# The RWKV-7 scans of a two-layer block: products with state and values on quarters of the array, a state update in two parts, and another order of the pieces

## The chip, the cores and the metric

One core of one Trainium2 chip runs the whole block: an RWKV-7 mixer (layer 0), then a differential-attention mixer (layer 1), over 2048 latent tokens and 256 context tokens of width 1024, all in float32. The metric is the device time of the launch in microseconds (us). The engines in the text are TensorE (PE; its weight loads are the rows PEld), VectorE (DVE), ScalarE (ACT), GpSimd (POOL) and SyncE (SP), whose queue issues most DMAs.

## The reference, cut to the scans

```python
def wkv_scan(r, w, k, v, kk, a, s0, reverse):
    def step(S, inp):                                   # per head: S is 64 x 64
        r_t, w_t, k_t, v_t, kk_t, a_t = inp
        sa = jnp.einsum("bhvk,bhk->bhv", S, kk_t)
        S = (S * w_t[:, :, None, :] - sa[..., None] * (kk_t * a_t)[:, :, None, :]
             + v_t[..., None] * k_t[:, :, None, :])
        return S, jnp.einsum("bhvk,bhk->bhv", S, r_t)
    s_fin, o = lax.scan(step, s0, xs, reverse=reverse)
...
    oc_f, sc_f = scan_direction(con, 0, s0, False)      # context, forwards and backwards
    oc_b, sc_b = scan_direction(con, 1, s0, True)
    ol_f, _ = scan_direction(lat, 0, sc_f, False)       # latents, from the context's final states
    ol_b, _ = scan_direction(lat, 1, sc_b, True)
    y = rwkv7_readout(ol_f + ol_b, lat, r_k, gn_g, gn_b, w_out, h.dtype)
```

There are 16 heads of width 64, two directions, and 2304 tokens in each scan.

## The kernel before, in words

`phase1` (to about 1150 us) projects and writes per-chunk operands to HBM, `phase2` (about 1168 to 2355 us) does the scans, and the readout, the attention and the output projection follow. Only `phase2` is touched.

A scan is done in 36 chunks of 64 tokens, both directions in step, so that each chunk has 32 head-and-direction problems of 64x64 blocks. Partitions 0-63 are `LO`, 64-127 `HI`; `half[d]` is the half of direction d, `other[d]` the other one. The loop `for m in range(nch + LEAD)` does the part of chunk m that needs no state, and the part with the state, `chain`, for chunk i = m - 5:

- `products` (L669) multiplies keys and queries of chunk m, 64x64 weights, 128 columns, on the four quarters of the array in turn. `scores_k` masks two such blocks into `KS` (DVE, L676), `scores_b` copies `A` (ACT, L681) and masks `Pb` (DVE, L682). Each call fills both banks of the pool `sc`.
- `invert` turns the 32x32 diagonal blocks of `A`, for a pair of chunks: four transposes on DVE (L692), then 30 elimination steps on GpSimd (L699, L700). `unpack` transposes the result back on DVE; `join_rows` (L728) and `join` (L744) build the full inverse `U` on TensorE, after a negation of `Dg` on DVE (L737). Their results pass through `sc` banks and are copied by ACT (L730, L746).
- `chain` stage 1 (L766): `KS` times the values, 128 columns of weights, into one bank for each head half and direction (`x00` to `x11`). Stage 2 (L775): queries times the state `St`, added in the same banks, and four ACT copies into `RS` (L783). Stage 3 (L790): `U` times that, with four ACT negations (L794). Stage 4 (L802): the keys turned by `turned` (L754) times the whole column of `RS`, 128 rows of weights, and DVE adds and decays the state (L804, L805). Stage 5 (L811): `Pb` times the result, four ACT copies (L814), DMA out.
- `seen` (L768) is a DVE copy of one element: other rows of the array add to the same banks in stage 2, so the first product there waits for it.

PE, DVE, ACT and POOL run in the order in which the program is written (`in_order`); SP's order is the scheduler's. Odd i and even i differ: for odd i the inverse of the next pair is unpacked and `join_rows` runs, for even i the two `join`s finish and `A` of a new pair is inverted. So the program repeats every two chunks. From m = 36 on there are no scores, and `fill` puts pieces of another product between the stages.

Of the kernel before, what the change touches and what calls it, by code (L numbers as in the profile page):

```python
# [612 lines left out]
def phase2(k):  # L613
# [9 lines left out]
    with ExitStack() as st:  # L623
# [5 lines left out]
        pp = pool("p2p", LEAD)  # L629
# [3 lines left out]
        rp = pool("p2r", 2)  # L633
        sc = pool("p2sc", 2, space=PSUM)
        xo = pool("p2xo", 1, space=PSUM)
# [3 lines left out]
        U = cx.tile([128, 32, 64], F32, name="U")  # L639
        St = cx.tile([128, 2, NPAIR, 64], F32, name="St")  # L640
# [11 lines left out]
        def values(i):  # L652

            RS = []
            for d in range(2):
                t = rp.tile([128, 16, 64], F32, name=f"RS{d}")
                n = ORDER[d][i]
                nc.sync.dma_start(out=t[other[d]], in_=S["v"][64 * n:64 * n + 64].rearrange("t (h v) -> t h v", v=64))
                RS.append(t)
            return RS  # L660

# [24 lines left out]
        def invert(A, eng):  # L686

            N = ip.tile([128, 32, 32], F32, name="N", bufs=2)
            for g in range(4):
# [7 lines left out]
            for m in range(1, 31):  # L697
                t = ip.tile([128, 31 - m, m], F32, name="rank1")
                eng.tensor_tensor(t, bcast(N[:, m + 1:32, m], 2, m), bcast(N[:, m, 0:m], 1, 31 - m), op=ALU.mult)  # L699
                eng.tensor_tensor(N[:, m + 1:32, 0:m], N[:, m + 1:32, 0:m], t, op=ALU.subtract)  # L700
                if eng is nc.vector and m % 5 == 0:
                    yield
            nc.gpsimd.memset(N.rearrange("p i j -> p (i j)")[:, 0:1024:33], -1.0)
            yield N

# [13 lines left out]
        joint = lambda: (sc if more else ch).tile([128, 16, 32], F32, name="scps" if more else "chps")  # L719
# [37 lines left out]
        def chain(i, QR, KS, Pb, RS, KB):  # L757
# [3 lines left out]
            px = [[xo.tile([128, 8, 64], F32, name=f"x{ab}{d}") for d in range(2)] for ab in range(2)]  # L761
            for p in range(8):
                for ab in range(2):
                    for d in range(2):
                        h = 8 * ab + p
# [5 lines left out]
            QR = both(QR, i)  # L771
            for d in range(2):
                for p in range(8):
                    for ab in range(2):
                        nc.tensor.matmul(px[ab][d][:, p], f2(QR[d][half[ab], p]), St[half[ab], d, p], start=False,  # L775
                                         stop=False, skip_group_check=True)
                        if (d, p, ab) == (0, 0, 0):
                            k.tc.add_manual_dep(
                                nc.cur_bb.bb.instructions[-1], before.name,
                                mybir.DependencyInfo(mybir.DependencyClass.Sync, mybir.DependencyReason.DATA),  # L780
                                reason="other rows of the array have added to the same banks")
                for ab in range(2):
                    nc.scalar.copy(RS[d][half[d], 8 * ab:8 * ab + 8], px[ab][d][LO])  # L783
            yield
            pa = [ch.tile([128, 8, 64], F32, name="chps") for _ in range(2)]
            for ab in range(2):
                for p in range(8):
                    for d in range(2):
                        h = 8 * ab + p
                        nc.tensor.matmul(pa[ab][half[d], p], U[half[d], 16 * par + h], RS[d][half[d], h], start=(p == 0),  # L790
                                         stop=True, skip_group_check=True)
            for d in range(2):
                for ab in range(2):
                    nc.scalar.mul(RS[d][half[d], 8 * ab:8 * ab + 8], pa[ab][half[d]], -1.0)  # L794
            yield
            if not last:
                KB = both(KB, i)
                for d in range(2):
                    ps = ch.tile([128, 8, 64], F32, name="chps")
                    for p in range(8):  # L800
                        for ab in range(2):
                            nc.tensor.matmul(ps[half[ab], p], KB[d][:, p, ab], RS[d][:, 8 * ab + p], start=(p == 0),  # L802
                                             stop=True, skip_group_check=True)
                    nc.vector.tensor_tensor(St[:, d], ps, St[:, d], op=ALU.add)  # L804
                    nc.vector.tensor_tensor(St[:, d], St[:, d], bcast(k.dec[:, d, ORDER[d][i]], 2, 64), op=ALU.mult)  # L805
            yield
            for ab in range(2):
                for p in range(8):
                    for d in range(2):
                        h = 8 * ab + p  # L810
                        nc.tensor.matmul(px[ab][d][HI, p], Pb[half[d], h], RS[d][half[d], h], start=False, stop=True,  # L811
                                         skip_group_check=True)
                for d in range(2):
                    nc.scalar.copy(RS[d][other[d], 8 * ab:8 * ab + 8], px[ab][d][HI])  # L814
            for d in range(2):
                n = ORDER[d][i]
                (nc.sync if i + 2 < NCH else nc.scalar).dma_start(
                    out=S["o"][d, 64 * n:64 * n + 64].rearrange("t (h v) -> t h v", v=64), in_=RS[d][other[d]])
# [5 lines left out]
        QR, KS, Pb, BK, BT, RS, KB, A = {}, {}, {}, {}, {}, {}, {}, {}  # L824
# [7 lines left out]
        turn = itertools.cycle((("RS0", rp), ("RS1", rp)))  # L832

        def spare():

            name, pool = next(turn)
            return pool.tile([128, D], F32, name=name)
# [5 lines left out]
        banks = itertools.cycle(f"x{ab}{d}" for ab in range(2) for d in range(2))  # L843

        def modulations(parts, space, pool, name):

            bank = lambda: pool.tile([128, 512], F32, name=name())
# [4 lines left out]
        if k.mod:  # L852
            mods = [modulations(((0, 4, 6), (1, 4, 6)), spare, xo, lambda: next(banks)),
                    modulations(((1, 0, 4),), free, sc, lambda: "scps")]
        inv0, unp, joins, N, chains = none, none, [none, none], {}, {}

        def first(A):
            for N[0] in invert(A, nc.vector):
                yield

        with in_order(k, mybir.EngineType.PE, mybir.EngineType.DVE, mybir.EngineType.Activation, mybir.EngineType.Pool):
            for m in range(nch + LEAD):
# [22 lines left out]
                if 0 <= i + 1 < nch:  # L885
                    RS[i + 1] = values(i + 1)
# [8 lines left out]
                odd = i >= 0 and i % 2 == 0  # L895
                if even:
# [4 lines left out]
                if more:  # L901
                    KS[m] = kp.tile([128, 16, 2, 64], F32, name="KS")
                    scores_k(0, both(BK, m), both(QR, m), KS[m])
# [4 lines left out]
                if more:  # L908
                    scores_k(1, both(BK, m), both(QR, m), KS[m])
                fill()  # L910
                if even:
# [3 lines left out]
                step(c)  # L915
                fill()
# [7 lines left out]
                if more:  # L924
                    if par == 0:
                        A[g] = ip.tile([128, 32, 64], F32, name="A", bufs=2)
                    Pb[m] = pp.tile([128, 16, 64], F32, name="Pb")
                    scores_b(0, both(BK, m), both(QR, m), A[g], Pb[m], par)
                if even:
                    step(unp)  # L930
                turn_keys(0)
                fill()
                if more:
                    scores_b(1, both(BK, m), both(QR, m), A[g], Pb[m], par)
# [7 lines left out]
                if 0 <= i + 1 < nch:  # L942
                    chains[i + 1] = chain(i + 1, QR, KS.pop(i + 1), Pb.pop(i + 1), RS.pop(i + 1), KB)
                    step(chains[i + 1])
                turn_keys(1)
                if more and par == 1:
                    if g == 0:
                        inv0 = first(A[0])
                    else:
                        for N[g] in invert(A[g], nc.gpsimd):  # L950
# [771 lines left out]
```

## Time and profile before

| | |
|---|---|
| median of 3 runs | 5145.27 us (5145.12 to 5148.8) |
| profiled execution | 5129.72 us, its span 5128.0 us |
| scans, first product to last chunk | 1168 to 2355 us |
| PE busy in the span | 92% |
| mean granted TensorE clock | 0.941 of full speed, 0.85 from 1400 to 2200 us |

A row of the profile gives an engine's busy time, its operation and tiles, and in brackets how long the engine was idle ahead of it and what released it. On PE one product in float32 is two rows, each with a weight load, so "x64" is 32 products; the text calls such a load and product a pair. A PEld row shows best when pairs are issued, since the rows of PE overlap.

### The profile page before, as it was taken

The numbers are of one execution on the slowest core, as the hardware profiler recorded it, in microseconds if no ns is written. First come the engines' busy times: TensorE is split into PE (matmuls) and PEld (weight loads), VectorE is DVE, ScalarE is ACT, GpSimd is POOL, SyncE is SP. The second block draws the span as 40 slices with busy tenths as digits, with TensorE's granted clock in tenths as the row PEclk, the third lists the DMA queues.
The fourth block names the chain that finished last, engine by engine and source line by source line (L and its number), as shares of the span: only waits on it lengthen the run. The fifth ranks groups of instructions, "written<-read, shape, count | busy, mean of one in ns | idle before, by whom it ended". The sixth has DMA issues, their size and how long they took to land. (4 is left out here: it accounts for less than half of the span.)

```text
span 5128.0 us, 103635 instructions
## 1 busy us (share of the span) xinstructions
PE 4706.2 (92%) x43090; PEld 4207.0 (82%) x43090; DVE 3582.4 (70%) x5478; ACT 2452.0 (48%) x4170; POOL 1458.2 (28%) x1809
## 2 busy tenths in 40 slices
PE   7999999994888888896878999998999999999999
PEld 5999999992878787875667888887888988888887
DVE  6778777774555555556887628517899989899853
ACT  5555555550434444343333122215777777777730
POOL 1221112111555555551331112113233223223310
PEclk8999999996888888898889999998999999999999
DMA  4565564555444444455654232231110111010042
GB/s 169 159 185 169 165 186 150 174 156 190 139 145 139 137 134 140 145 153 184 209 185 144 97 125 93 99 105 33 28 35 27 28 44 35 10 44 17 9 152 91
DMA packets 610965, 593.39 MB, mean 116 GB/s; under 512 B 27014, under 2 KB 525113, under 8 KB 609473
## 3 DMA queue, kind: packets, MB, share of 16 engines
q1 hardware_dynamic: 608337, 584.15, 36.8%
q8 instruction: 340, 5.57, 0.5%
q10 hardware_dynamic: 2160, 2.62, 0.2%
q14 instruction: 128, 1.05, 0.1%
HBM read 386.91 MB, written 199.77 MB: 114 GB/s over the span
## 5 line engine op out<-in xcount | busy, mean ns | idle before, releaser
L1454 ACT ACTIVATE p<-p,m 128x2304 f32<-128x2304 f32 x256 | 568.8, 2222 | 203.2 <-DVE p L1443 200.9
L1486 PE MATMUL pv<-v,at 128*128 128x128 f32 x4608 | 626.5, 277 | 6.3 <-ACT at L1481 4.6
L1486 PEld LDWEIGHTS pv<-v,at 128*128 128x128 f32 x4608 | 564.3, 192 | 16.1 <-ACT at L1481 12.9
L1440 PE MATMUL sc<-ks,qh 128*128 128x512 f32 (+1 forms) x1280 | 520.6, 407 | 15.3 <-DVE p L1443 15.2
L1441 PE MATMUL sc<-ks,ql 128*128 128x512 f32 (+1 forms) x1280 | 464.2, 372 | 0.3 <-POOL ql L1421 0.3
L363 PE MATMUL mmps<-hH,wH 128*128 128x386 f32 x1632 | 432.6, 345 | 19.1 <-DVE sg L574 12.8
L1464 DVE SCALAR_TENSOR_TENSOR p<-p,r,p 128x1152 f32<-128x1152 f32 x256 | 427.1, 1669 | 4.5
L363 PE MATMUL mmps<-hL,wH 128*128 128x386 f32 x1632 | 428.1, 342 | 2.1 <-DVE hL L92 2.1
L1481 ACT COPY at<-tps 128x512 f32<-128x512 f32 (+1 forms) x640 | 345.2, 540 | 177.4 <-PE tps L1479 174.0
L363 PE MATMUL mmps<-hH,wL 128*128 128x386 f32 x1632 | 427.1, 342 | 1.2 <-DVE nm_ss L197 0.8
L967 PE MATMUL mmps<-wH,hH 128*128 128x512 f32 x1088 | 425.0, 391 | 3.1 <-ACT hH L91 3.1
L967 PE MATMUL mmps<-wL,hH 128*128 128x512 f32 x1088 | 424.8, 390 | 0.0
L967 PE MATMUL mmps<-wH,hL 128*128 128x512 f32 x1088 | 424.3, 390 | 0.0
L1443 DVE TENSOR_SCALAR_CACHE_REDUCE p<-sc,m 128x1280 f32<-128x1280 f32 x256 | 395.6, 1545 | 18.0 <-PE sc L1441 1.4
L1421 POOL TENSOR_TENSOR ql<-qt,qh 128x256 fp32r<-128x256 f32 x128 | 112.2, 877 | 979.1 <-ACT qt L1420 917.8
L1479 PE MATMUL tps<-ident,p 128*128 128x128 f32 x2304 | 361.8, 275 | 10.6 <-ACT qt L1420 5.0
L669 PE MATMUL scps<-QR,BK 64*64 64x128 f32 x4608 | 250.1, 332 | 125.2 <-DVE KS L676 31.4
L1443 DVE TENSOR_SCALAR_CACHE_REDUCE p<-sc 128x1024 f32<-128x1024 f32 x256 | 311.7, 1218 | 56.7 <-PE sc L1441 55.6
L669 PEld LDWEIGHTS scps<-QR,BK 64*64 64x64 f32 x4608 | 185.9, 166 | 176.6 <-DVE KS L676 41.7
L1479 PEld LDWEIGHTS tps<-ident,p 128*128 128x128 f32 x2304 | 273.1, 141 | 61.3 <-ACT at L1481 11.7
L363 PEld LDWEIGHTS mmps<-hH,wH 128*128 128x128 f32 x1632 | 299.2, 192 | 24.9 <-DVE sg L574 16.3
L363 PEld LDWEIGHTS mmps<-hH,wL 128*128 128x128 f32 x1632 | 302.3, 191 | 2.1 <-DVE wL L92 2.0
(296 smaller groups left out, 10427.4 us busy)
## 6 DMA issues: line engine op xcount, KB each, us to landing
wr<-in_rw_in_dram SPq DMA_DIRECT2D x102, 512.0 KB
s_qr<-QR SPq DMA_DIRECT2D x48, 768.0 KB
QR<-s_qr SPq DMA_DIRECT2D x72, 512.0 KB
BK<-s_bk SPq DMA_DIRECT2D x72, 512.0 KB
BT<-s_bk SPq DMA_DIRECT2D x72, 512.0 KB
s_bk<-BK SPq DMA_DIRECT2D x47, 768.0 KB
wraw<-in_da_in_dram SPq DMA_DIRECT2D x64, 512.0 KB
RS<-s_v SPq DMA_DIRECT2D x72, 256.0 KB
```

What stands on the lines that cost most here:

```text
L363: nc.tensor.matmul(a[:, :b1 - b0], wt[:, kt, :], ht[:, kt, b0:b1], start=(kt == 0 and wt is wH and ht is hH), stop=(kt == KT - 1 and last))
L669: nc.tensor.matmul(f2(out[ab][(other if key else half)[d], j]), BK[d][rows, p, 1 - d if key else d], f2(QR[d][rows, p]), start=(j == 0), s ...
L967: k.nc.tensor.matmul(ps, s(kt), m(kt), start=(kt == 0 and s is sH and m is mH), stop=(kt == KT - 1 and last))
L1421: nc.gpsimd.tensor_tensor(ql, qt, qh.bitcast(F32), op=ALU.subtract)
L1440: nc.tensor.matmul(s[:, b0 - g0:b1 - g0], qh[:, cs], ks, start=True, stop=False)
L1441: nc.tensor.matmul(s[:, b0 - g0:b1 - g0], ql[:, cs], ks, start=False, stop=True)
L1443: nc.vector.tensor_scalar(tiles[n][c][:, g0:g1], s[:, :g1 - g0], -1.0, m, op0=ALU.mult, op1=ALU.min, accum_out=least)
L1454: nc.scalar.activation(P, P, AF.Exp, bias=m, scale=-1.0, accum_out=z)
L1464: nc.vector.scalar_tensor_tensor(P0[:, b0:b1], P1[:, b0:b1], r, P0[:, b0:b1], op0=ALU.mult, op1=ALU.add)
L1479: nc.tensor.transpose(ps[:, c - b0:c - b0 + 128], P0[:, c:c + 128], k.ident)
L1481: (eng.copy if eng is nc.scalar else eng.tensor_copy)(at[b][:, :b1 - b0], ps[:, :b1 - b0])
L1486: nc.tensor.matmul(acc, at[b][:, c - b0:c - b0 + 128], H.v[:, c // 128], start=(c == 0), stop=(c == T - 128))
```

## The change

- Stages 1 and 2 take 64 columns of weights at a time (`slot` 0 and 1), so that four quarters of the array are in use in turn. The banks are by head half and by slot: `px` (pool `xp`, rows `half[d]`, the part that goes on) and `po` (pool `op`, rows `other[d]`, the output). Two ACT copies of 128 partitions go to a new tile `RU`.
- Stage 4 takes 64 rows of weights at a time, in two parts: with the values, ahead of stage 3, and with `RU`, after it. It uses the two `xps` banks that `px` has left, which stage 1 of the next chunk takes again.
- `RS0`, `RS1` become one tile `RV` of two buffers; ACT does the three evacuations in two copies each instead of four.
- The negation of `Dg` goes from DVE to ACT. The joins always use `ch` banks.
- In odd m `scores_b` is now ahead of `scores_k`, `invert` starts in mid-iteration with its transposes spread out, and its first four elimination steps are on DVE.

```diff
         def invert(A, eng):
...
-                    yield
+                    yield N
+            yield from eliminate(nc.vector, 1, 5)
+            yield from eliminate(eng, 5, 31)
             nc.gpsimd.affine_select(out=N, in_=N, pattern=[[1, 32], [-1, 32]], base=-1, channel_multiplier=0,
...
-        joint = lambda: (sc if more else ch).tile([128, 16, 32], F32, name="scps" if more else "chps")
+        joint = lambda: ch.tile([128, 16, 32], F32, name="chps")
...
-                nc.vector.tensor_scalar(U[r, cs, 32 * (g % 2):32 * (g % 2) + 32], Dg[r, cs], -1.0, None,
-                                        op0=ALU.mult)
+                nc.scalar.mul(U[r, cs, 32 * (g % 2):32 * (g % 2) + 32], Dg[r, cs], -1.0)
...
-                        nc.tensor.matmul(px[ab][d][:, p], f2(KS[other[d], h]), RS[d][other[d], h], start=(p == 0),
-                                         stop=False, skip_group_check=True)
-            nc.vector.tensor_copy(seen, px[1][1][:, 7, 0:1])
+                        add(t[ab][rows[d], p], KS[other[d], h, slot], RV[other[d], h], p == 0, False)
+            nc.vector.tensor_copy(seen, po[1][:, 7, 0:1])
...
+            for slot, (t, rows) in enumerate(((px, half), (po, other))):
                 for p in range(8):
+                    for d in range(2):
+                        for ab in range(2):
+                            add(t[ab][rows[d], p], QR[i, d][half[ab], p, slot], St[half[ab], d, p], False, slot == 0)
...
+                if slot == 0:
                     for ab in range(2):
+                        nc.scalar.copy(RU[:, 8 * ab:8 * ab + 8], px[ab])
+            yield
+            if not last:
+                pS = [xp.tile([128, 8, 64], F32, name="xps") for _ in range(2)]
+                for p, ab, h in heads:
+                    for d in range(2):
+                        add(pS[d][half[ab], p], KB[i, d][other[d], p, ab], RV[other[d], h], p == 0, False)
...
             if not last:
-                KB = both(KB, i)
+                for p, ab, h in heads:
+                    for d in range(2):
+                        add(pS[d][half[ab], p], KB[i, d][half[d], p, ab], RU[half[d], h], False, True)
...
+                    rest = [lambda q=q: scores_b(q, *args, A[g], Pb[m], par) for q in range(2)]
+                    order = rest + keys if par else keys + rest
```

On PE, stage 1 of a chunk before (`x` are its banks, `RS` the values; one row is one product):

```order
L669 MATMUL scps_16298<-QR_15540,BK_15833 64x128
L766 MATMUL x00_16326<-RS0_15984,KS_14270 128x64
L766 MATMUL x01_16327<-RS1_15986,KS_14270 128x64
L766 MATMUL x10_16328<-RS0_15984,KS_14270 128x64
L766 MATMUL x11_16329<-RS1_15986,KS_14270 128x64
```

and the same stage in the changed kernel, where every product of the chain stands at L765:

```order
L669 MATMUL scps_22481<-QR_21606,BK_21931 64x128
L765 MATMUL xps_22509<-RV_22110,KS_20069 64x64 x2
L765 MATMUL ops0_22511<-RV_22110,KS_20069 64x64 x2
L765 MATMUL xps_22510<-RV_22110,KS_20069 64x64 x2
L765 MATMUL ops1_22512<-RV_22110,KS_20069 64x64 x2
```

Each product of 128 columns has become two of 64, the two directions (x2) into one bank, and the two slots into different banks.

On ACT, an even i before, from the copies of stage 2 to those behind the second `join`:

```order
L783 COPY RS_16864<-x_17206 64x512
L783 COPY RS_16864<-x_17208 64x512
L783 COPY RS_16866<-x_17207 64x512
L783 COPY RS_16866<-x_17209 64x512
L746 COPY U<-scps 32x16x32 x2
L794 ACTIVATE RS_16864<-chps 64x512 x2
L794 ACTIVATE RS_16866<-chps 64x512 x2
L814 COPY RS_16864<-x_17206 64x512
L814 COPY RS_16866<-x_17207 64x512
L814 COPY RS_16864<-x_17208 64x512
L814 COPY RS_16866<-x_17209 64x512
L746 COPY U<-scps 32x16x32 x2
```

and in the changed kernel:

```order
L742 ACTIVATE U<-Dg 32x16x32 x4
L759 COPY KB_23636<-chps 128x512 x2
L790 COPY RU<-xps 128x512 x2
L750 COPY U<-chps 32x16x32 x2
L681 COPY A<-scps 128x256 x2
L803 ACTIVATE RU<-chps 128x512 x2
L681 COPY A<-scps 128x256 x2
L817 COPY RV<-ops_23569 128x512
L817 COPY RV<-ops_23570 128x512
L742 ACTIVATE U<-Dg 32x16x32 x4
L750 COPY U<-chps 32x16x32 x2
```

The three evacuations are two rows each, and the four negations stand behind the output's copies and ahead of `U`'s.

On DVE, an even i before, from the state's update to the next mask (`N` is the block to invert):

```order
L805 TENSOR_TENSOR St<-St,dec 128x512
L737 TENSOR_SCALAR U<-Dg 32x16x32 x4
L682 TENSOR_TENSOR Pb<-scps,causalP 128x256 x4
L768 COPY seen<-x_15838 128x1
L692 STREAM_TRANSPOSE N<-A 32x1024 x2
L692 STREAM_TRANSPOSE N<-A 32x32x32 x2
L676 TENSOR_TENSOR KS<-scps,causalK 128x512 x2
```

and in the changed kernel:

```order
L682 TENSOR_TENSOR Pb<-scps,causalP 128x256 x4
L701 STREAM_TRANSPOSE N<-A 32x1024
L810 TENSOR_TENSOR St<-xps,St 128x512
L811 TENSOR_TENSOR St<-St,dec 128x512
L810 TENSOR_TENSOR St<-xps,St 128x512
L811 TENSOR_TENSOR St<-St,dec 128x512
L701 STREAM_TRANSPOSE N<-A 32x1024
L676 TENSOR_TENSOR KS<-scps,causalK 128x512 x2
L701 STREAM_TRANSPOSE N<-A 32x32x32
L676 TENSOR_TENSOR KS<-scps,causalK 128x512 x2
L774 COPY seen<-ops_15588 128x1
L701 STREAM_TRANSPOSE N<-A 32x32x32
```

The four transposes no longer stand in a row, and the negation is gone from this queue.

## Rows read from the trace of the kernel before

**Rows 1.** Stretches: length, busy PE, PEld, DVE, ACT, POOL, granted clock, DMA share, GB/s.
```profile
1168.00:1287.00 119.00, 67.38 (x842) 39.07 (x842) 62.79 (x111) 11.60 (x28) 16.50 (x31) 0.64 0.48 166
1400.00:2200.00 800.00, 698.50 (x15505) 639.09 (x15499) 448.98 (x552) 329.66 (x632) 425.15 (x814) 0.85 0.46 140
1804.73:1808.38 3.65, 3.65 (x67) 3.65 (x64) 0.76 (x2) 0.65 (x2) 0.00 (x0) 1.00 0.69 185
1839.97:1846.88 6.91, 6.91 (x64) 6.90 (x64) 0.00 (x0) 1.06 (x2) 6.05 (x11) 0.50 0.38 132
2200.00:2355.00 155.00, 139.87 (x2827) 116.50 (x2825) 60.32 (x76) 68.37 (x125) 54.24 (x103) 0.91 0.51 156
```

**Rows 2.** Groups by line and shape, 1400 to 2200 us: busy, mean ns, idle before.
```profile
L775 PEld LDWEIGHTS x<-St,QR 64*128 64x128 f32 x1664 | 118.1, 227 | 28.0 <-DVE seen L768 25.8 <-issue 2.2
L737 DVE TENSOR_SCALAR U<-Dg 32x512 f32<-32x512 f32 x104 | 59.6, 573 | 1.9
L814 ACT COPY RS<-x 64x512 f32<-64x512 f32 x105 | 61.0, 581 | 97.6 <-PE x L811 95.7
```

**Rows 3.** Blocks of one kind, from the timeline: start, duration, pairs, at the granted clock there.
```profile
1801.35 0.86 PEld L669 LDWEIGHTS scps<-QR,BK 64*64 64x64 f32 x30 [1.14 <-ACT U L746]
1802.38 0.86 PEld L754 LDWEIGHTS chps<-ident,BT 128*128 128x128 f32 x8 [0.17 <-issue]
1804.73 3.65 PEld L766 LDWEIGHTS x<-RS,KS 64*128 64x128 f32 x64 [0.17 <-issue]
1809.47 3.65 PEld L775 LDWEIGHTS x<-St,QR 64*128 64x128 f32 x64 [0.17 <-issue]
1814.02 2.00 PEld L790 LDWEIGHTS chps<-RS,U 64*64 64x64 f32 x64
1824.78 2.10 PEld L728 LDWEIGHTS scps<-Tt,A 32*32 32x32 f32 x128
1839.97 6.91 PEld L775 LDWEIGHTS x<-St,QR 64*128 64x128 f32 x64 [1.97 <-DVE seen L768]
1858.15 1.95 PEld L811 LDWEIGHTS x<-RS,Pb 64*64 64x64 f32 x64
2250.04 1.95 PEld L802 LDWEIGHTS chps<-RS,KB 128*64 128x64 f32 x64 [1.34 <-ACT RS L794]
```

**Rows 4.** Who waited for whom, 1400 to 2200 us: total us, times, longest.
```profile
PEld scps L669 <- ACT U L746: 28.5, 26, 1.1
PEld scps L669 <- DVE KS L676: 26.2, 26, 1.6
PEld x L775 <- DVE seen L768: 25.8, 13, 2.1
PEld scps L669 <- ACT Tt L730: 21.9, 25, 1.1
PEld scps L744 <- PE x L811: 11.2, 13, 0.9
PEld chps L802 <- ACT RS L794: 9.6, 13, 0.7
PEld scps L744 <- DVE U L737: 3.3, 13, 0.3
POOL N L695 <- DVE N L692: 313.1, 13, 26.7
```

**Rows 5.** The second join of an even i, from the timeline.
```profile
1859.33 2.40 ACT L814 COPY RS<-x 64x512 f32<-64x512 f32 x4 [2.76 <-PE x L811]
1860.00 1.74 DVE L737 TENSOR_SCALAR U<-Dg 32x512 f32<-32x512 f32 x4
1860.95 0.14 PEld L744 LDWEIGHTS scps<-U,Tt 32*32 32x32 f32 x2 [0.86 <-PE x L811]
```

More of the change, by code (lines that the diff above doesn't have):

```diff
@@ L755, in turned, with chain @@
                 nc.scalar.copy(KB[:, 4 * q:4 * q + 4], ps.rearrange("p j (a c) -> p j a c", a=2))
-        def chain(i, QR, KS, Pb, RS, KB):
+        def chain(i, QR, KS, Pb, RV, KB):
             last = i + 1 == NCH
             par = i % 2
-            px = [[xo.tile([128, 8, 64], F32, name=f"x{ab}{d}") for d in range(2)] for ab in range(2)]
-            for p in range(8):
-                for ab in range(2):
+            add = lambda out, lhsT, rhs, start, stop: nc.tensor.matmul(out, lhsT, rhs, start=start, stop=stop,
+                                                                        skip_group_check=True)
+            heads = [(p, ab, 8 * ab + p) for p in range(8) for ab in range(2)]
+            px = [xp.tile([128, 8, 64], F32, name="xps") for _ in range(2)]
+            po = [op.tile([128, 8, 64], F32, name=f"ops{ab}") for ab in range(2)]
+            for p, ab, h in heads:
+                for slot, (t, rows) in enumerate(((px, half), (po, other))):
@@ L770, in chain @@
             yield
-            QR = both(QR, i)
-            for d in range(2):
+            for slot, (t, rows) in enumerate(((px, half), (po, other))):
                 for p in range(8):
-                    for ab in range(2):
[L775 to L783, printed above, removed]
@@ L784, in chain @@
-            yield
+                    for d in range(2):
+                        for ab in range(2):
+                            add(t[ab][rows[d], p], QR[i, d][half[ab], p, slot], St[half[ab], d, p], False, slot == 0)
+                            if before:
+                                k.tc.add_manual_dep(
+                                    nc.cur_bb.bb.instructions[-1], before.name,
+                                    mybir.DependencyInfo(mybir.DependencyClass.Sync, mybir.DependencyReason.DATA),
+                                    reason="other rows of the array have added to the same banks")
+                                before = None
@@ L810, in chain @@
                         h = 8 * ab + p
[L811 to L814, printed above, removed]
+                        add(po[ab][other[d], p], Pb[half[d], h], RU[half[d], h], False, True)
+                nc.scalar.copy(RV[:, 8 * ab:8 * ab + 8], po[ab])
             for d in range(2):
@@ L831, in phase2 @@
         both = lambda t, i: [t[i, d] for d in range(2)]
-        turn = itertools.cycle((("RS0", rp), ("RS1", rp)))
         def spare():
-            name, pool = next(turn)
-            return pool.tile([128, D], F32, name=name)
+            return rp.tile([128, D], F32, name="RV")
         def free():
             return bp.tile([128, D], F32, name="BK")
-        banks = itertools.cycle(f"x{ab}{d}" for ab in range(2) for d in range(2))
         def modulations(parts, space, pool, name):
-            bank = lambda: pool.tile([128, 512], F32, name=name())
+            bank = lambda: pool.tile([128, 512], F32, name=name)
             for layer, lo, hi in parts:
@@ L852, in phase2 @@
         if k.mod:
-            mods = [modulations(((0, 4, 6), (1, 4, 6)), spare, xo, lambda: next(banks)),
-                    modulations(((1, 0, 4),), free, sc, lambda: "scps")]
+            mods = [modulations(((0, 4, 6), (1, 4, 6)), spare, xp, "xps"),
+                    modulations(((1, 0, 4),), free, sc, "scps")]
         inv0, unp, joins, N, chains = none, none, [none, none], {}, {}
-        def first(A):
-            for N[0] in invert(A, nc.vector):
-                yield
         with in_order(k, mybir.EngineType.PE, mybir.EngineType.DVE, mybir.EngineType.Activation, mybir.EngineType.Pool):
@@ L895, in phase2 @@
                 odd = i >= 0 and i % 2 == 0
+                if more:
+                    KS[m] = kp.tile([128, 16, 2, 64], F32, name="KS")
+                    Pb[m] = pp.tile([128, 16, 64], F32, name="Pb")
+                    if par == 0:
+                        A[g] = ip.tile([128, 32, 64], F32, name="A", bufs=2)
+                    args = both(BK, m), both(QR, m)
+                    keys = [lambda q=q: scores_k(q, *args, KS[m]) for q in range(2)]
+                    rest = [lambda q=q: scores_b(q, *args, A[g], Pb[m], par) for q in range(2)]
+                    order = rest + keys if par else keys + rest
+                else:
+                    order = [lambda: None] * 4
                 if even:
@@ L900, in phase2 @@
                     step(joins[0])
-                if more:
-                    KS[m] = kp.tile([128, 16, 2, 64], F32, name="KS")
-                    scores_k(0, both(BK, m), both(QR, m), KS[m])
+                order[0]()
                 fill()
@@ L907, in phase2 @@
                 step(c)
-                if more:
-                    scores_k(1, both(BK, m), both(QR, m), KS[m])
+                order[1]()
                 fill()
+                if more and par == 1:
+                    inv = invert(A[g], nc.gpsimd if g else nc.vector)
+                    N[g] = step(inv)
                 if even:
@@ L914, in phase2 @@
                 fill()
-                step(c)
-                fill()
+                if more and par == 1:
+                    step(inv)
                 if even:
@@ L923, in phase2 @@
                     step(joins[1])
[L924 to L928, printed above, removed]
+                order[2]()
                 if even:
                     step(unp)
+                if more and par == 1:
+                    step(inv)
                 turn_keys(0)
                 fill()
+                order[3]()
                 if more:
-                    scores_b(1, both(BK, m), both(QR, m), A[g], Pb[m], par)
                     for d in range(2):
@@ L947, in phase2 @@
                     if g == 0:
-                        inv0 = first(A[0])
+                        inv0 = inv
                     else:
-                        for N[g] in invert(A[g], nc.gpsimd):
+                        for _ in inv:
                             pass
```

52 lines of the change are left out of this document (22 added, 30 removed).

## The prediction

> **What bounds the kernel now.** I read the stretches first. From 1400 to 2200 us PE is busy for 698.5 of 800 us, VectorE for 449, ScalarE for 330, GpSimd for 425, and DMA for a share of 0.46 [rows 1]. So the scans are PE's, with two leaks: PE idles for 12% of the time, and its granted clock is 0.85. The groups give the period: 1664 pairs of stage 2 are 26 chunks of 64 pairs, so a chunk takes 800/26 = 30.8 us [rows 2].
>
> Then I read what such a chunk is made of. [...] The sum is 20.7 us. The seven waits of the load queue add up to 126.5 us in 26 chunks, which is 4.9 us each [rows 4]. [...] That makes 30.2; the other 0.6 us are short idles at changes of shape. The reader is to see that two thirds of a chunk is issuing, and that the waits and the clock share the rest.
>
> **What the products on quarters change.** What sets a block's length is how many parts of the array work at a time. With 64 columns of weights, 64 pairs take 2.00 us in stage 3 (two row halves, one bank), 1.95 in stage 5 (the same), and 1.95 in stage 4 (two column halves) [rows 3]: two at a time, so a quarter needs 2 x 1.95/64 = 61 ns per pair. The scores show four at a time: 30 pairs of twice the moving columns take 0.86 us, 29 ns each, which is 115 ns for a quarter [rows 3]; two at a time that would be some 57 ns. Four quarters at 61 ns make 15.2 ns per pair. No row has four quarters at 64 moving columns. The bounds are 15.2 and the 30.5 ns of two at a time. I take 15.2: 128 pairs of joins go in 2.10 us, 16.4 ns each [rows 3], so issuing at that rate is shown.
>
> Stages 1, 2 and 4 go from 64 pairs each to 128, so from 3.65 + 3.65 + 1.95 = 9.25 us to 3 x 1.95 = 5.85 us. That takes 3.4 us off a chunk, and 17.3 us of issuing are left. That stage 4's first half runs ahead of stage 3 costs nothing more, as it is in this count. Its new wait, for `xps` banks that ScalarE must have emptied, is covered by the second slot and a block of scores (0.98 + 0.92 us against two copies of 0.58 [rows 2]).
>
> [...]
>
> **What the order and the queues change, per chunk.** (a) Scores waited for `U` and `Tt`, since the joins used their banks: 28.5 + 21.9 us in 26 chunks, 1.9 each [rows 4]. The joins now use `ch`, whose next user stands behind a block of scores. I take 0. If that cover were too short, the uncovered part of a second copy of 0.58 would return. (b) The waits for `KS` and for `seen`, 1.0 each [rows 4], stay: VectorE's transposes are spread out, but PE arrives earlier. (c) Stage 4's wait of 9.6/26 = 0.4 falls to 0.2, as one negation is left behind stage 3 where there were three. (d) The second join of an even i gets a longer wait. Now VectorE negates beside ScalarE's output copies, and PE waits 0.86 us [rows 5], 14.5 us in all, 0.6 a chunk [rows 4]. In the changed queue ScalarE first makes the last output copy (0.58) and then three negations that the product needs. ScalarE's price for these isn't in the trace; VectorE's are 0.44 (four in 1.74 us [rows 5]) to 0.573 [rows 2], and a copy of 512 columns on ScalarE is 0.58. With 0.3 for the product to land that is 2.2 to 2.6 us, so 1.3 a chunk. PE has nothing to do meanwhile; behind the join stand scores and the turned keys. (e) `join_rows` waits for two transposes of `unpack`, which now come late since PE is ahead: between 0 and one transpose (2 us in two chunks, about 1.0 a chunk). I take 0.3, nearest to today's nothing. (f) The four elimination steps on VectorE, the new RV buffers and the early start of `invert` are on engines with room: GpSimd waits 313 of 800 us for its transposes [rows 4]. Their cover is VectorE's idle 44%; without it the steps would add to (b). DMA goes from a share of 0.46 to about 0.55, and stays hidden unless a key block, loaded as the last scores end, takes longer than what PE does until the next scores, some 4.8 us (1.95 + 0.86 + 1.95).
>
> The waits then are 1.0 + 1.0 + 0.2 + 1.3 + 0.3 = 3.8 us.
>
> **The sum.** (17.3 + 3.8 + 0.6) / 0.85 = 25.5 us, 5.2 less than the 30.7 of today. The clock stays at 0.85 in it, since issuing and waiting shrink alike: waits were 5.5 of 26.2 us at full clock and will be 4.4 of 21.7. There are 31 chunks with scores: 161 us. The last five (155 us in [rows 1], with the clock at 0.91) save 3.4 less the longer join wait, 2.6 each: 13 us. The first five iterations (119 us, where PE is busy for 67) have no `chain`; I leave them. So 174 us go. The profiled execution took 5129.7 us (its span 5128.0 and 1.7 around it), 15.5 under the median of 5145.3; 5129.7 - 174 = 4956, and with that distance **4970 us**.
>
> **The rivals.** *The clock falls.* [...] At a mean of 0.75 a chunk is 21.7/0.75 = 28.9 us, and the gain 1.8 x 31 + 13 = 69 us: 5076. For it speaks that the clock falls here after stretches with waits (0.85 against 0.91 in the end [rows 1]); against it that the share of waits falls from 21% to 20%. *The waits go.* If the spread transposes take `KS` and `seen` away, (b) and (e) are 0.8 in place of 2.3 and the clock may rise to 0.92: (17.3 + 2.3 + 0.6)/0.92 = 22.0, so 5145 - 8.7 x 31 - 13 = 4862. *Only two quarters at a time (slower).* If the quarters of one row half take turns, the pair costs 30.5 ns, the three stages 11.7 us, 2.5 more than before, and with today's waits all 36 chunks lose 2.5/0.85 = 2.9: 5145 + 106 = 5251. With my waits (1.1 fewer) it is 1.6 a chunk, 5204. At my waits it decides from (9.25 + 1.1)/384 = 27 ns a pair. For it speaks that no row has four quarters at 64 columns, and that both row halves now write to one bank in stage 1; against it that stage 3 does that at 2.00 us, where stage 4, from one row range, takes 1.95 [rows 3]. [...] *ScalarE's queue binds.* If each join and each evacuation waits behind negations, and (d) doubles and (e) reaches its bound, the waits are 5.8 and a chunk (17.3 + 5.8 + 0.6)/0.85 = 27.9 us; the gain is 2.8 x 31 + 13 = 100 us: 5045.
>
> **How the numbers follow.** My forecast holds with 0.6 (4920 to 5010, by 24 to 27 us a chunk), the falling clock 0.11, the waits going 0.12, ScalarE's queue 0.10, two at a time 0.07. The range leaves out the slower case and the far end of the good one: 4885 to 5080. A difference of 0.2%, 10 us, is about what a measurement here can tell from none: faster 0.91, the same 0.03 (27 ns a pair or near), slower 0.06.
>
> **What would show it.** In the changed profile 64 pairs of a quartered stage should take about 1 us in the load queue at full clock, 2 us if I am wrong. Scores should no longer wait for `U` or `Tt`, and the second join should wait some 2.5 us for ScalarE's negation once in two chunks. The chunk should be 25.5 us, the clock near 0.85, and the last five chunks about 2.6 us shorter each. A pair at 27 ns or more, or a clock under 0.75, makes the prediction wrong, and so does a wait for loads of `BK`, of which the trace has none from 1400 us on.

## The result, and the profile after

The changed kernel takes 5063.45 us (median of 4 runs, 5055.34 to 5065.65) against 5145.19 for the kernel before on the same chip (4 runs), a ratio of 0.9838 with a 95% interval of 0.9821 to 0.9855. That is 82 us less, in the direction of the forecast and inside its range, but less than half of the 175 us forecast. The profiled execution has a span of 5053.6 us.

The stretches, with the columns of [rows 1]:

```profile
1168.00:1287.00 119.00, 70.68 (x1298) 44.50 (x1296) 66.12 (x122) 19.73 (x44) 29.47 (x53) 0.71 0.49 161
1400.00:2200.00 800.00, 619.56 (x21738) 565.66 (x21730) 442.58 (x577) 325.91 (x608) 412.65 (x753) 0.87 0.50 149
2200.00:2355.00 155.00, 98.57 (x2091) 75.66 (x2086) 78.35 (x111) 52.28 (x83) 19.62 (x13) 0.80 0.58 181
```

From 1400 to 2200 us PE is busy for 620 us, where it was 699, in which it does 40% more products; so it idles for 180 us, where it idled for 101. The waits of its load queue in that stretch, with the columns of [rows 4], say for what:

```profile
PEld xps L765 <- issue: 49.7, 57, 3.2
PEld ops L765 <- issue: 48.4, 28, 5.6
PEld chps L748 <- ACT U L742: 36.7, 28, 2.1
PEld scps L669 <- issue: 29.4, 30, 4.0
PEld chps L748 <- issue: 16.0, 6, 3.5
PEld chps L758 <- issue: 13.0, 29, 2.4
PEld chps L733 <- issue: 7.5, 9, 1.6
PEld xps L765 <- DVE seen L774: 7.0, 8, 1.0
PEld scps L669 <- DVE KS L676: 1.6, 8, 0.3
```

The scores' waits for `U` and `Tt` [rows 4] are gone, those for `KS` and `seen` nearly. In their place stands "issue": PE waits for nothing that the profile can name, for 169 us in all, single times for 5.6. The timeline shows where (start, duration, pairs, idle before):

```profile
1801.95 0.73 PEld L669 LDWEIGHTS scps<-QR,BK 64*64 64x64 f32 x25 [1.34 <-issue]
1802.55 1.11 PEld L765 LDWEIGHTS xps<-RU,KB 64*64 64x64 f32 x63
...
1803.60 1.19 PEld L765 LDWEIGHTS ops<-RU,Pb 64*64 64x64 f32 x37
1805.97 0.83 PEld L765 LDWEIGHTS ops<-RU,Pb 64*64 64x64 f32 x25 [1.18 <-issue]
1808.90 0.18 PEld L748 LDWEIGHTS chps<-U,Tt 32*32 32x32 f32 x2 [2.11 <-ACT U L742]
```

63 pairs of a quartered stage take 1.11 us at a granted clock of 1.00, close to the forecast (64 in about 1 us). But the stops for "issue" stand in the middle of blocks, between pairs that depend on nothing new.

The first row below is the last output copy ahead of that join, the second the negation behind it (ScalarE's timeline, against [rows 5]):

```profile
1806.97 0.58 ACT L817 COPY RV<-ops 128x512 f32<-128x512 f32 x1 [1.64 <-PE ops L765]
1807.58 2.57 ACT L742 ACTIVATE U<-Dg 32x512 f32<-32x512 f32 x4
```

The next table puts the main profiled runs side by side. A chunk is a 31st of the time from the first stage 1 to the 32nd; the granted clock and the "issue" idles of the load queue are those from 1400 to 2000 us, the idles divided by the chunks in them. The ratio is to the kernel before on the same chip.

| kernel | ratio, 95% | first stage 1 | chunk us | "issue" us a chunk | clock |
|---|---|---|---|---|---|
| before | 1 | 1286.9 | 30.65 | 1.0 | 0.85 |
| changed | 0.984 (0.982-0.986) | 1270.6 | 28.71 | 6.1 | 0.86 |
| order only | 0.964 (0.961-0.967) | 1263.4 | 25.69 | 0.9 | 0.96 |
| quarters only | 0.998 (0.997-1.000) | 1287.5 | 30.06 | 4.9 | 0.85 |
| changed, stage 4 whole | 0.971 (0.969-0.974) | 1270.4 | 26.64 | 4.3 | 0.92 |
| changed, earlier negation | 0.976 (0.974-0.978) | 1275.2 | 27.47 | 5.8 | 0.90 |
| changed, two quarters at a time | 0.988 (0.985-0.990) | 1267.3 | 29.14 | 3.7 | 0.94 |
| changed, more traffic | 0.994 (0.991-0.996) | 1279.5 | 30.15 | 6.8 | 0.85 |
| order only, more traffic | 0.974 (0.972-0.977) | 1265.6 | 26.88 | 1.9 | 0.93 |

Of the 74 us in the span, 16 come before the first stage 1, 60 from the 31 chunks; the four chunks after them, which run without scores, lose 7 (102.6 us before, 109.3 after), and the rest of the program gains the remainder.

### The profile page after: what moved, and what is told of

Its sections match the earlier page's. It is cut to its first block, busy times and chain, and to the rows that moved or that the text cites. A ratio compares the mean times of both kernels' runs of the same rounds, so it can differ in the third digit from the quotient of the medians.

```text
span 5053.6 us, 117000 instructions
## 1 busy us (share of the span) xinstructions
PE 4542.8 (90%) x49938; PEld 4055.6 (80%) x49938; DVE 3536.9 (70%) x5470; ACT 2422.7 (48%) x4098; POOL 1412.2 (28%) x1673
## 5 line engine op out<-in xcount | busy, mean ns | idle before, releaser
L1443 PE MATMUL sc<-ks,qh 128*128 128x512 f32 (+1 forms) x1280 | 520.1, 406 | 15.3 <-DVE p L1446 15.2
L693 POOL TENSOR_TENSOR rank<-N 128x130 f32<-128x130 f32 (+14 forms) x442 | 234.2, 530 | 419.8 <-DVE N L694 386.5
L363 PEld LDWEIGHTS mmps<-hL,wH 128*128 128x128 f32 x1632 | 299.9, 190 | 3.3 <-DVE hL L92 3.1
```

Of the source, the lines that this page charges most:

```text
L363: nc.tensor.matmul(a[:, :b1 - b0], wt[:, kt, :], ht[:, kt, b0:b1], start=(kt == 0 and wt is wH and ht is hH), stop=(kt == KT - 1 and last))
L1443: nc.tensor.matmul(s[:, b0 - g0:b1 - g0], qh[:, cs], ks, start=True, stop=False)
```

## The experiments

**One part at a time.** The order only: the changed kernel with `chain` as before, on `RS` and the four `x` banks.

```diff
-                        add(t[ab][rows[d], p], KS[other[d], h, slot], RV[other[d], h], p == 0, False)
+                        nc.tensor.matmul(px[ab][d][:, p], f2(KS[other[d], h]), RS[d][other[d], h], start=(p == 0),
+                                         stop=False, skip_group_check=True)
```

> The new order, the joins' banks and ScalarE's negation of Dg, with stages 1, 2 and 4 whole as before (592 pairs a chunk instead of 784). Theory S (the engine runs out of instructions: in the changed kernel PE idles 126.5 us of 600 for nothing that the profile names, 6.0 us in each of 21 chunks, and a chunk of 784 pairs takes 28.7 us, 36.6 ns a pair): 592 pairs at 36.6 ns are 21.7 us, so the instructions hardly bind here; the waits that went (1.9 for U and Tt, less 0.7 more for Dg) come off, a chunk is 30.65 - 1.2/0.85 = 29.2 us, the prefix gains the same 16 us, and the whole is about 5145 - 45 - 16 = 5085, ratio 0.988 to the kernel before. Rival R (the quarters gave their 3.4/0.85 = 4.0 us a chunk and the new order or the longer ScalarE queue took 2 us of it back): this kernel is slower than before by 2 x 31 - 16 = 46 us, ratio 1.009.

Measured: 4957 us, some 100 us faster than the whole change (differences between runs are taken by the ratios). The rival is refuted, and the plain gain was three times what was expected: without the quarters the rest of the change is worth 184 us. Its stretch from 1400 to 2000 us and its waits there:

```profile
1400.00:2000.00 600.00, 545.56 (x13982) 504.08 (x13980) 373.09 (x496) 352.51 (x661) 354.91 (x648) 0.96 0.55 167
```

```profile
PEld chps L748 <- ACT U L742: 38.3, 22, 3.0
PEld chps L806 <- ACT RS L798: 16.7, 24, 0.7
PEld scps L669 <- issue: 5.9, 20, 0.6
PEld chps L758 <- issue: 5.5, 22, 0.3
PEld scps L669 <- DVE Pb L682: 3.9, 11, 0.4
```

No wait for `KS` or `seen` is left, and the clock is 0.96. The quarters only: the kernel before with `chain` of the changed one.

> The quarters and the state in two parts, with the order, the joins' banks and VectorE's negation of before. Theory S: 784 pairs a chunk at 36.6 ns are 28.7 us, and the waits of before (4.9 us a chunk) only partly let the stream catch up; of the 4.0 us a chunk that the faster issuing is worth, at most about half is left: a chunk of 29.0 to 31, ratio 0.99 to 1.00. Rival R: the quarters alone give 4.0 x 36 = 144 us, ratio 0.972.

Measured: ratio 0.998, as theory S had it: the quarters alone are worth 11 us. Its waits, 1400 to 2000 us, hold most of the "issue" idles of the changed kernel (4.9 us a chunk) and waits of the kernel before:

```profile
PEld xps L761 <- DVE seen L770: 32.4, 10, 4.2
PEld xps L761 <- issue: 22.6, 29, 2.3
PEld scps L669 <- ACT U L746: 22.0, 20, 1.1
PEld ops L761 <- issue: 20.1, 16, 3.2
```

Stage 4 whole in the changed kernel, with values and `RU` in one tile a direction:

```diff
-                        add(pS[d][half[ab], p], KB[i, d][half[d], p, ab], RU[half[d], h], False, True)
+                        add(pS[d][half[ab], p], KB[i, d][:, p, ab], RV[d][:, h], p == 0, True)
```

> The changed kernel with stage 4 whole again: 64 pairs over all 128 rows instead of 128 pairs on quarters, 720 pairs a chunk instead of 784; values and corrected values stand in one tile a direction, which costs ScalarE two more negations of half the rows a chunk. By the rates of the rows stage 4 takes 1.95 us either way. Theory S: 64 pairs x 36.6 ns = 2.3 us a chunk less, 0.3 back for the two negations: 5063 - 2.0 x 31 = 5001, ratio to the kernel before 0.972 (the changed kernel has 0.984). Rival R (the number of instructions does not matter): 0.984 or up to 0.988, as the values part no longer covers the copies of stage 2.

Measured: 4993 us, ratio 0.971. Sixty-four pairs fewer a chunk, at the same time of issuing, take 2.1 us off it, 1.7 of them as "issue" idles; the clock is 0.92 in place of 0.86.

**The disputed cost by itself.** A program of products alone. Its quarters are

```python
        def quarters(n):
            for c in range(n):
                for r in range(2):
                    for d in range(2):
                        mm(banks[2 * r + d][half[d], c % 8], W[half[r], c % 16], V[half[r], c % 16])
...
        quarters(768)
```

> Leaves the whole computation out and writes zeros. PE only: 1024 pairs of 128 columns, then 6144 pairs on quarters with 64 columns with no data moving, 1024 wide pairs again, 3072 pairs on two row halves, 1024 wide pairs, and 6144 pairs on quarters while 32 MB of loads of 2 MB each run. Theory S in its plain form: the quarters without loads already take 25 to 37 ns a pair, with idle time put down to issue; with loads more, and the halves (30.5 ns by their rate) are held up little. Rival D (only data traffic delays the fetch): 15.2 ns a pair without loads, some 93 us in all, and 30 ns or more with loads. Rival R: 15.2 ns in both.

The load queue, first where no data move, from the end of the wide pairs on:

```profile
3.05 57.37 PEld L99 LDWEIGHTS w<-V,W 64*64 64x64 f32 x1023 [3.05 <-DVE V L94]
...
60.30 3.50 PEld L99 LDWEIGHTS b<-V,W 64*64 64x64 f32 x223
64.90 1.96 PEld L99 LDWEIGHTS b<-V,W 64*64 64x64 f32 x128 [1.10 <-issue]
68.90 1.96 PEld L99 LDWEIGHTS b<-V,W 64*64 64x64 f32 x128 [2.04 <-issue]
72.90 1.96 PEld L99 LDWEIGHTS b<-V,W 64*64 64x64 f32 x128 [2.04 <-issue]
...
106.18 1.96 PEld L99 LDWEIGHTS b<-V,W 64*64 64x64 f32 x128 [1.50 <-issue]
```

and then while the loads run:

```profile
440.71 1.96 PEld L99 LDWEIGHTS b<-V,W 64*64 64x64 f32 x128 [1.50 <-issue]
446.92 3.29 PEld L99 LDWEIGHTS b<-V,W 64*64 64x64 f32 x128 [4.25 <-issue]
453.14 3.39 PEld L99 LDWEIGHTS b<-V,W 64*64 64x64 f32 x128 [2.92 <-issue]
```

The DMA queues from 100 to 200 us (packets, MB, share):

```profile
q8 instruction: 28, 0.46, 2.0%
```

The reader is to see the counts. After the first 224 pairs each run is exactly 128 pairs, issued in 1.96 us (15.3 ns a pair), and each starts on average 3.75 us after the one before (64.90 to 106.18 us are 11 of them). Meanwhile the queue of instructions brings 28 packets of 16 KB in 100 us, one in 3.6 us. So PE eats 128 pairs, 256 instructions, in half of the time in which the next 256 arrive. Beside loads at 407 GB/s the starts are 6.2 us apart. The two row halves issue without a gap, 3052 pairs in 89 us, 29 ns each. Theory S holds in its plain form, and loads add to it. Little stands ready: the first stop comes 224 pairs behind the wide ones in quiet and 96 behind them beside the loads, though the wide pairs had taken 56 ns each (1023 in 57.37 us).

The changed kernel's own trace shows the same stops. From 1400 to 2200 us its instruction queue brings

```profile
q8 instruction: 170, 2.79, 1.5%
```

which is 6.1 packets a chunk, as many as 784 pairs fill (2 x 784/256); the 43468 rows of PE and PEld in that stretch are 256 to a packet. From 1400 to 2000 us it has 56 "issue" idles of more than 0.6 us, 105 of the 126.5 us in all. Of these, 55 end 1.0 to 1.8 us after such a packet has ended, as all 94 of the dense program do (1.2 to 1.6 us), though the packets are 4.7 us apart; and all but two of them follow the one before by a multiple of 128 pairs, to within 3. The shorter idles, 21 us, are not put down to the fetch by this.

**Does a wait elsewhere give the time back?** The negation of `Dg` for the second join is queued ahead of `chain`'s last step.

```diff
+                if odd:
+                    step(joins[1])
                 step(c)
                 fill()
...
                 if odd:
                     step(joins[1])
-                    step(joins[1])
```

> The new order with whole stages (4957 us, ratio 0.964), and the second join's negation of Dg put on ScalarE's queue one step earlier, ahead of chain's last step. In the order-only trace PE waits 38.3 us of 600 for this negation, 1.6 us in each of 23.4 chunks. Theory S (592 pairs a chunk leave the instruction stream slack): nearly all of it comes off: 1.4 x 31 = 43 us, some 4914, ratio 0.956. If the stream binds here too, it is 4945 or more, ratio over 0.962.

> The changed kernel (ratio 0.984) with the same edit. In its trace the wait is 28.8 us of 600, 1.4 a chunk. Theory S: PE then only waits elsewhere for instructions, since 784 pairs take 28.7 us whatever the waits: 0 to 15 us gained, ratio 0.981 to 0.984. Rival A (ScalarE's queue is what ate the gain): 1.4 x 31 = 43 us gained or more, ratio 0.975.

Measured: 0.962 (0.958 to 0.967) with the order only, which can't be told from 0.964, and 0.976 (0.974 to 0.978) in the changed kernel, some 40 us and so what rival A had. Both expectations of theory S fell. In the first the wait for `Dg` went and the next one came up, as its waits (1400 to 2000 us) say:

```profile
PEld scps L669 <- DVE KS L676: 17.6, 22, 1.4
PEld chps L806 <- ACT RS L798: 16.1, 23, 0.7
```

In the second the "issue" idles stayed at 5.8 us a chunk, and there too `KS` came up, 24.5 us where it was 1.0:

```profile
PEld scps L669 <- DVE KS L676: 24.5, 22, 2.5
```

So rival A has the time, but only in part by its wait: PE idles 7.5 us a chunk where it idled 8.1, and the other half of the 1.2 us that a chunk is shorter goes with the clock, 0.90 in place of 0.86. Still, 784 pairs do not take 28.7 us whatever the waits: the total of pairs in a chunk does not set its time. The theory had to become local (theory L in what follows): the fetch is at most about a block ahead, so a pause elsewhere saves nothing for the next run of small pairs. That lead is the author's estimate, and the dense program's first stops agree: 96 pairs behind the wide ones beside the loads, and 224 in quiet, of which at 128 in 3.75 us some 120 can have come in the 3.50 us that they took.

**The same pairs, half as fast.**

```diff
-            for p, ab, h in heads:
-                for slot, (t, rows) in enumerate(((px, half), (po, other))):
+            for slot, (t, rows) in enumerate(((px, half), (po, other))):
+                for p, ab, h in heads:
```

(and the same for stages 2 and 4.)

> The changed kernel with the same matmuls, but each quartered stage takes its quarters two at a time (loops turned, so that next to each other stand pairs of two quarters only). By the rows a pair then costs 30.5 ns instead of 15.2: 384 pairs a chunk take 11.7 us instead of 5.85. Theory L (a run of small pairs outruns the fetch, which brings 128 pairs in 3.7 us and stands at most a block ahead, so that each quartered block of 128 pairs costs 1.95 us of issuing and at least 1.8 of stall): at 3.9 us a block hardly a stall is left: a chunk changes by 5.85 less the 5.0 us of issue idles that the quarters brought, under 1 us, and the granted clock rises as PE idles less: within 30 us of the changed kernel, ratio 0.978 to 0.990, issue idles in 600 us from 126.5 to under 50. Rival R (the rate of the quarters sets the time): 5.85/0.9 = 6.5 us a chunk slower, 200 us and more, ratio over 1.02.

Measured: 5079 us, ratio 0.988. Doubling the time of a quartered pair costs some 20 us in the whole program where its rate would make it 200. One stage and the stretch:

```profile
1819.06 1.89 PEld L765 LDWEIGHTS xps<-RV,KS 64*64 64x64 f32 x60
```

```profile
1400.00:2000.00 600.00, 517.10 (x16207) 485.90 (x16204) 335.20 (x438) 243.04 (x457) 296.57 (x540) 0.94 0.50 148
```

60 pairs take 1.89 us, the "issue" idles fall from 126.5 to 75.8 us in 600 (not under 50, as expected), and the clock rises from 0.86 to 0.94. This is the sharpest test: 5.85 us more of issuing a chunk cost 0.4 (29.14 against 28.71), so the rate is not what counts. Theory L has the time right, but the idles give back only 2.4 us a chunk and the other waits 0.4; the rest, some 2.6, goes by difference with the clock, for which it had no price.

**Does data traffic slow the fetch here too?** Each chunk gets two copies of 512 KB between scratch tensors. In the first try the scheduler of SP's queue had moved them into the program's first part, so the scans' traffic did not change (149 and 151 GB/s in the changed kernel, 167 and 168 in the order only) and nothing was tested; the ratios were 0.985 and 0.969.

> The changed kernel with 1 MB of copies between scratch tensors added to each chunk (its own traffic is 149 GB/s x 28.7 us = 4.3 MB). In the dense kernel a block of 128 pairs took 3.5 to 4.0 us to come in quiet and 6.0 to 6.6 us beside loads at 408 GB/s. Theory S: the share of DMA goes from 0.50 to about 0.62, a block of 128 pairs from some 4.7 us to 5.0, and 6.1 blocks a chunk make 1.5 to 2.0 us: 45 to 70 us slower than the changed kernel, ratio 0.993 to 0.998, with the idle put down to issue. Rival (fetch does not depend on data traffic): 0.984.

> The order-only kernel (ratio 0.964) with the same copies. Theory S: 4.6 blocks of 128 pairs at 5.0 us are 23.2 us, under its chunk of 25.7: 0 to 20 us slower, ratio 0.964 to 0.968, much less than the changed kernel loses. If data that come late were the cause, both would lose the same, and PE would wait for BK, QR or RS.

In the second the copies wait for the products in front of them.

```diff
+            nc.sync.dma_start(out=S["pad"][d, i % 4], in_=S["bk"][d, 0])
+            for engine, x in last.items():
+                k.tc.add_manual_dep(nc.cur_bb.bb.instructions[-1], x.name,
+                                    mybir.DependencyInfo(sync, mybir.DependencyReason.DATA), reason="place")
```

> Again the changed kernel with 1 MB of copies between scratch tensors a chunk, this time tied to their place (in the first try they had moved into the first stage of the program, so nothing was tested). Theory L with a fetch that data slow down (a block in 3.5 to 4.0 us quiet, 6.0 to 6.6 beside loads at 408 GB/s): the share of DMA goes from 0.50 to about 0.62 and the stalls grow by 0.12 x 2.6 x 6.1 = 1.9 us a chunk, 30 to 60 us on the changed kernel: ratio 0.990 to 0.996. If data traffic does not matter: 0.984.

> The order-only kernel (0.964) with the same tied copies. Theory L: whole pairs leave time for the fetch, the stalls stay near 1 us a chunk, 0 to 20 us slower: ratio 0.964 to 0.968. If late data were the cause, it loses as much as the changed kernel, and PE waits for BK, QR or RS.

Now the traffic went from 149 to 178 GB/s in the changed kernel and from 167 to 196 in the order only. Measured: 50 us for the changed kernel, as expected, though its "issue" idles grew by 0.8 us a chunk and not by 1.9; but as much for the order only (0.974 against 0.964), where at most 20 us were. The order only does not wait for late data, though:

```profile
PEld chps L748 <- ACT U L742: 38.4, 22, 3.0
PEld chps L806 <- ACT RS L798: 15.3, 21, 0.7
PEld scps L669 <- issue: 13.2, 21, 3.3
PEld chps L733 <- issue: 8.6, 9, 2.1
PEld x L814 <- issue: 4.1, 3, 2.1
```

Its own runs of small pairs (scores, joins, stage 5) now stop for instructions: the "issue" idles are 1.9 us a chunk where they were 0.9, and 16 of them are longer than 0.6 us where one was. Traffic delays the fetch in both kernels; that whole stages leave it slack was wrong.

**What the order gives.** Three kernels split it: the kernel before with the joins in `ch` banks alone, the order only with the joins in `sc` banks, and the order only with the negation on VectorE.

```diff
-        joint = lambda: (sc if more else ch).tile([128, 16, 32], F32, name="scps" if more else "chps")
+        joint = lambda: ch.tile([128, 16, 32], F32, name="chps")
```

> The kernel before with one line changed: the joins' products go into the banks named chps. Forecast's step (a): the scores' waits for U and Tt (37.2 us of 600, 1.9 us in each of 19.6 chunks) go, and nothing else: 1.9/0.85 x 31 = 69 us, ratio 0.986. If PE then only meets the next wait (KS, seen) earlier: ratio 0.995 or more.

> The order-only kernel (ratio 0.964) with the joins' products in the scores' banks as before. If the banks are what the order gains by: the scores wait for U and Tt again, 1.9 us a chunk, and the granted clock falls from 0.96 towards 0.85: ratio 0.980 or more. If the order (the pieces and VectorE's work spread out) takes the waits for KS and seen away by itself: ratio 0.970 to 0.976, clock over 0.9.

> The order-only kernel with the negation of Dg on VectorE as before. Step (d) of the forecast: on ScalarE it costs 1.6 us of wait a chunk against 0.6 before, so this is 0.7 to 1.0 x 31 = 20 to 30 us faster than order only, ratio 0.958 to 0.960; if VectorE, which evacuates KS, is then late, as it was with the earlier negation, 0.962 to 0.966.

Measured: 0.983 (0.981 to 0.985), 0.980 (0.978 to 0.983) and 0.989 (0.986 to 0.992). The banks alone give 93 us, with `KS` and `seen` waited for as before and the clock at 0.90; the order without them gives 110, with next to no wait for `KS` or `seen` (0.8 us of 600), those for `U` and `Tt` back, and 0.91. Together they make 184. The third came out on the wrong side: VectorE's negation costs 128 us more than ScalarE's. Its timeline says why, and the wait that follows:

```profile
1596.71 1.89 DVE L701 STREAM_TRANSPOSE N<-A 32x1024 f32<-32x1024 f32 x1
1598.62 1.75 DVE L742 TENSOR_SCALAR U<-Dg 32x512 f32<-32x512 f32 x4
```

```profile
PE chps L749 <- DVE U L742: 49.1, 10, 4.9
```

In the new order VectorE has the state's update and a transpose ahead of the negation, and PE waits 4.9 us for it in every second chunk.

**A better version?** The order only with the earlier negation and all elimination steps on GpSimd.

```diff
-            yield from eliminate(nc.vector, 1, 5)
-            yield from eliminate(eng, 5, 31)
+            yield from eliminate(eng, 1, 31)
```

> Order only with the earlier negation (ratio 0.962), and all steps of the elimination on GpSimd. There PE waits 17.6 us of 600 for VectorE's KS, 0.76 a chunk, which came in place of the wait for Dg. If VectorE's four steps stand in KS's way: 0.5 to 0.8 x 31 = 15 to 25 us come off, ratio 0.957 to 0.959. If the spread transposes do, nothing changes: 0.962.

Measured: 0.966 (0.964 to 0.969), and PE still waits 18.9 us of 600 for `KS`; the steps don't stand in its way. The order only, with (4935 us) or without (4957 us) the earlier negation, beats both kernels and is the best found.

## Why the prediction was right and wrong

**The rate of the quarters** was right: 15.3 ns a pair in the dense program where 15.2 were taken. The rival of two quarters at a time, with 30.5 ns, fell. The 17.3 us of issuing are the blocks of [rows 3], all at a granted clock of 1.00, 3.67 + 3.65 + 3.65 + 2.00 + 1.95 + 1.95 + 1.72 + 2.10 = 20.7, less the 3.4 of the three stages.

**The step that failed** is the 0.6 us of "short idles at changes of shape" that went unchanged into the sum, (17.3 + 3.8 + 0.6)/0.85. They became 6.1 us a chunk (the kernel before has 1.0 in the same count). No row shows the 0.6: it is what 20.7 us of issuing, 4.9 of waits and 0.15 x 30.8 = 4.6 for the clock of 0.85 leave of a chunk. The sum took issuing as free of what feeds it. Its evidence, the joins' 128 pairs in 2.10 us [rows 3], was one run of 128 pairs, shorter than the 224 that the dense program issued in quiet before its first stop; a chunk has three such blocks more. In the dense program a block costs 1.96 us of issuing and 1.5 to 2.0 of stall, so by an estimate from these figures three of them take some 11.2 us, where the whole stages took 9.25, and the quarters lose 1.9 us a chunk at full clock. The traces say much the same: against the order only, issuing is 3.4 us less and the "issue" idles are 5.2 us more, a loss of 1.8. Other waits are 0.8 less, and by difference some 2 of the 3.0 us by which the changed kernel is behind (28.71 against 25.69) go with its lower clock. Put right in this term and in the waits (2.0 us), the forecast's own sum is (17.3 + 2.0 + 6.1)/0.86 = 29.5 us, where 28.71 were measured. The time lies between two rivals, the falling clock (5076) and ScalarE's queue (5045), but neither is what happened: the clock did not fall, and (d) did not double.

**The waits** came out lower than forecast. (a) was right. (b) was wrong: `KS` and `seen` were kept at 1.0 us each a chunk, and 1.6 and 7.0 us in 27.9 chunks are left; here the rival "the waits go" was right. (c) and (e) are small, as forecast. (d) was right in size (the 0.3 us taken for a product to land is near the 0.22 to 0.37 that one of stage 5 lasts in the trace before): 36.7 us in 27.9 chunks, 1.3 each, and taking it away gave some 40 us, half of it with the clock. But it was booked as a price of moving to ScalarE, and the move pays in the new order.

**The clock** was kept at 0.85, and is 0.87 from 1400 to 2200 us. That this came out is luck: in the order only it is 0.96 from 1400 to 2000 us, and the quarters bring it down again, to 0.86 in that stretch. No run shows the rival's 0.75 there: the lowest was 0.84, in the order only with the negation on VectorE. In the order only the waits and idles are 3.7 us a chunk (86.5 of 600 us in 23.4 chunks) where they were 5.8, and 2.1 at the old clock would be 2.5 us; the chunk is 5.0 shorter, so about half of the order's gain goes with the clock, which the forecast held fixed. The two errors have opposite signs. The quarters were to give 4.0 us a chunk (3.4/0.85) and, on top of the order, took 3.0 (alone, on the kernel before, they gave 0.6, so the parts do not simply add); the order was to give 1.3 (1.1/0.85) and gave 5.0. Only the sum, 1.9 against 5.2, was seen at first.

**The ends**: the first iterations, left unchanged in the forecast, gained 16 us, which is the order's doing: stage 1 starts at 1263.4 us with the order only and at 1287.5 with the quarters only. The last chunks, forecast to save 13, lost 7 in four; these four take 111.5 us with the quarters only and 100.9 with the order only, but 113.1 with the banks alone, so what lengthens them stays open. Open too is by which path the traffic delays the fetch, and how the granted clock follows from the pattern of idle times; the runs show only both together.

## What to carry to other kernels

Cutting products into smaller ones that run side by side brought 11 us by itself here, where 3.4 us a chunk of issuing were saved: 128 pairs issue in 1.96 us where their instructions take 3.75 us to arrive in quiet and 6.2 beside loads at 407 GB/s. Count the pairs in each dense run, and compare these two times. The profile showed this limit as idle time on "issue" between products that wait for nothing, 6.1 us a chunk. Price each part of a change by a kernel of its own: here one part hid the loss of another, and half of the edit is worth more than twice the whole.

## What the runs showed that was not expected

- A float32 product on a quarter of the array issues at 15.3 ns a pair, but in a long run it averages 29 ns with no data moving (6144 pairs in 176 us).
- Loads at 407 GB/s stretch the arrival of 256 instructions from 3.75 to 6.2 us.
- Doubling the time of 384 pairs a chunk cost the kernel only some 20 us, as the stalls shrank and the granted clock rose from 0.86 to 0.94.
